# A hybrid decoder: the diagonal of linear attention from an elementwise product, the last output tile in two token halves, and dummy matmuls ahead of the first weights

## The chip, the cores and the metric

The kernel runs on one core of one Trainium2 chip. The metric is the device time of one launch in microseconds (us); lower is better. PE is the tensor engine, DVE the vector engine, ACT the scalar engine, SP the engine that issues most DMAs.

## What is computed

Two layers, each with two sub-layers on x (512 tokens, 1024 channels, float32), and a norm at the end:

```python
for l in range(DEPTH):                                   # DEPTH = 2
    x = x + hybrid_mixer(rmsnorm(x, norm1_w[l]), ...)    # SSD + gated linear attention + dilated attention
    x = x + conv_ffn(rmsnorm(x, norm2_w[l]), ...)        # up 1024 -> 2*2816, conv, SiLU gate, down 2816 -> 1024
return rmsnorm(x, final_norm_w)
```

The change touches two places of it. One is the gated linear attention (GLA): 4 heads with 64 key channels and 128 value channels, whose score for a token t and an earlier token s is the sum over the key channels of q[t] k[s] exp(b[t] - b[s]), b being the running sum of the log decays. For s = t the exponent is zero, so the diagonal of the scores is the plain product of q and k, summed over the 64 channels of the head. The other is the last FFN down-projection with the final norm: out[t] = x[t] * w / sqrt(mean(x[t]^2) + eps), where the mean runs over all 1024 channels.

## The kernel before

Channels lie on the 128 partitions and the 512 tokens on the free axis, so x is 8 tiles of 128x512 (`xs[m]`). Each float32 factor of a large product is split into a rounded part and a rest (`xh`, `xl` of the input, `wh`, `wl` of a weight), and each product is three matmuls, rounded by rounded, rounded by rest, rest by rounded: `mm3` puts them into a queue named `large`. `flush()` issues what the queue holds (L178). `mm()` (L186) and `transpose()` (L190) issue one small float32 matmul at once, and `follow()` then one large one (L183), so that small matmuls stand between large ones. PE's instructions stand in the order in which the program's text issues them; the other engines' order is set by a scheduler.

The weights come in units of 128x1024 (512 KB), 374 in all. `fetch` (L242) issues a unit's DMA on SP, up to 6 units ahead with 4 buffers; `parts` makes the rounded part on ACT (L249) and the rest on DVE (L251), up to 3 units ahead with 3 buffers. One unit is 24 large matmuls of 512 columns. `side()` registers a generator that goes on one step when a given number of units has been started; that is how attention, GLA and SSD are threaded between the projections.

GLA: `gla()` projects q and k for two pairs of heads (`gq`, `gk`, 128 channels are two heads of 64), then v and the output gate. `gla_pair()` (one for each pair, as a side) builds the score matrices `S` of the four 128-token blocks. Ahead of its levels it fills S with the diagonal: for each of two heads four matmuls k^T q over the 64 channels (8 of them a pair, 64 rows of PE in use), of which DVE keeps the diagonal by a multiply with the identity matrix (L620, 128x256, four a pair). Then nine levels follow. In a level, ACT makes decay factors (`ex`, L632), DVE multiplies q and k by them (`qsb`, `ksb`, L635 to L641), PE multiplies these (`mx<-qsb,ksb`), and DVE copies what belongs to the level into S (L649). Between the two pairs' groups of k^T q in layer 0 also four transposes of a 16-row tile `gd` stand on PE (L190), which SSD's decay needs.

The start: SP issues the DMAs of x's tiles and of the first weight units between them, then those of the constants. ACT makes `xh` of tile 0, after it has loaded its table, then `wh` of unit 0. PE runs three units of v projections, and then the sums `mx<-ones,acc` of the first norm, for which DVE has added up the squares of the eight x tiles in `acc` (L359), between the `wl` of the units and constants such as `lev`.

The end: the last loop makes the eight tiles of the down-projection, each 66 matmuls of 512 columns. Behind tile 7 come its two DVE steps (`dn`, then `x`), its square on ACT, sums on PE over the channels, the reciprocal root on DVE in 12 small instructions (`factors`), which also makes a diagonal matrix `dg` of the result; PE broadcasts it (`mx<-dg,ones`), DVE multiplies the eight tiles (L1069), and ACT and SP issue a DMA of 256 KB for each.

## Time and profile before

| | us |
|---|---|
| median of 3 runs (2321.18 to 2324.29) | 2322.52 |
| the profiled execution's own time | 2325.6 |
| its span, first to last instruction | 2323.8 |
| PE busy | 2300.8 (99%) |
| weight loads on PE | 1903.1 (82%) |
| DVE busy | 1420.4 (61%) |
| ACT busy | 917.6 (39%) |
| HBM traffic | 202.45 MB, 87 GB/s |

The mean granted clock of PE over the span is 0.995 of full speed. Busy times of PE are made of records that overlap, since matmuls are pipelined: what a matmul costs in a row of matmuls is the distance between two starts, and not the duration in its row. A float32 matmul is recorded as two (x2), since PE makes two passes for it. The rows are times in us from the start of the span; the bracket at a row's end is the idle time of its engine just ahead of it and what ended that.

### The profile page before, as it was taken

How to read it: one execution, taken by the hardware profiler on the slowest of the kernel's cores; microseconds unless marked ns; L12 is line 12 of the kernel's file. 1: busy time of each engine (PE TensorE's matmuls, PEld its weight loads, DVE VectorE, ACT ScalarE, POOL GpSimd, SP SyncE). 2: the span in 40 equal slices, each digit the busy share in tenths (PEclk: the TensorE clock that was granted, in tenths of full speed). 3: DMA queues.
4: the chain of work that ended last, by engine and by line, in shares of the span. 5: the costliest groups of instructions: out<-in, count | busy, mean ns of one | idle time of the engine just before them, and what ended most of it. 6: DMA issues, size and time to landing. Idle time of an engine off the chain costs nothing.

```text
span 2323.8 us, 27417 instructions
## 1 busy us (share of the span) xinstructions
PE 2300.8 (99%) x10776; PEld 1903.1 (82%) x10776; DVE 1420.4 (61%) x2527; ACT 917.6 (39%) x1503; POOL 0.2 (0%) x4
## 2 busy tenths in 40 slices
PE   8999999999999999999999999999999999999997
PEld 7888878888888888888888888788888888888886
DVE  5467548687865566654335764686888556665533
ACT  5354423445443333332244444234454433333321
POOL 0000000000000000000000000000000000000000
PEclk9999999999999999999999999999999999999998
DMA  5322222222223333333333222222222233323331
GB/s 182 105 77 82 73 64 87 78 72 73 82 73 100 92 99 95 96 100 94 97 91 100 83 82 73 71 84 73 73 73 82 82 95 96 97 94 100 98 93 54
DMA packets 58512, 204.21 MB, mean 88 GB/s; under 512 B 7152, under 2 KB 7824, under 8 KB 58384
## 3 DMA queue, kind: packets, MB, share of 16 engines
q1 hardware_dynamic: 57808, 201.42, 28.8%
q8 instruction: 84, 1.38, 0.2%
q10 hardware_dynamic: 576, 1.05, 0.1%
q14 instruction: 44, 0.36, 0.1%
HBM read 200.35 MB, written 2.10 MB: 87 GB/s over the span
## 4 chain that ended last, share of the span: by engine, by line
PE 98%; DVE 1%; ACT 0%; DMA 0%; issue 0%; DVEq 0%; SPq 0%; ACTq 0%
PE pp L178 77%; PE pp L183 11%; PE mx L186 8%; PE mx L190 2%; DVE wl L251 0%; DVE x L1069 0%; DVE cv L775 0%; DMA x<-in_xT 0%; DVE xD L834 0%; DVE th L918 0%; DVE th L943 0%; DVE xdt L833 0%; DVE xe L836 0%; ACT cx L778 0%; ACT L350 0%
## 5 line engine op out<-in xcount | busy, mean ns | idle before, releaser
L249 ACT CAST wh<-raw 128x1024 fp32r<-128x1024 f32 x374 | 393.1, 1051 | 952.7 <-PE pp L178 727.9
L251 DVE TENSOR_TENSOR wl<-raw,wh 128x1024 fp32r<-128x1024 f32 x374 | 457.4, 1223 | 355.6 <-ACT wh L249 350.1
L178 PE MATMUL pp<-xh,wl 128*128 128x512 f32 x1582 | 617.7, 390 | 0.0
L178 PE MATMUL pp<-xl,wh 128*128 128x512 f32 x1556 | 607.0, 390 | 0.0
L178 PE MATMUL pp<-xh,wh 128*128 128x512 f32 x1504 | 587.8, 391 | 0.0
L178 PEld LDWEIGHTS pp<-xh,wl 128*128 128x128 f32 x1582 | 297.7, 188 | 63.5 <-issue 1.0
L178 PEld LDWEIGHTS pp<-xl,wh 128*128 128x128 f32 x1556 | 293.1, 188 | 60.5 <-issue 0.5
L178 PEld LDWEIGHTS pp<-xh,wh 128*128 128x128 f32 x1504 | 283.3, 188 | 60.4 <-DVE wl L251 1.5
L183 PE MATMUL pp<-xh,wh 128*128 128x512 f32 x304 | 148.3, 488 | 0.0
L178 PE MATMUL pp<-hh,wl 128*128 128x512 f32 x352 | 136.9, 389 | 0.0
L178 PE MATMUL pp<-hh,wh 128*128 128x512 f32 x352 | 136.9, 389 | 0.0
L178 PE MATMUL pp<-hl,wh 128*128 128x512 f32 x352 | 136.9, 389 | 0.0
L771 DVE TENSOR_TENSOR cx<-pp,rstdB 128x512 f32<-128x512 f32 x76 | 52.3, 689 | 121.1 <-PE pp L178 121.0
L183 PE MATMUL pp<-xl,wh 128*128 128x512 f32 x252 | 124.6, 495 | 0.0
L183 PE MATMUL pp<-xh,wl 128*128 128x512 f32 x226 | 111.4, 493 | 0.0
L178 PE MATMUL pp<-wh,xh 128*128 128x512 f32 x245 | 96.3, 393 | 7.9 <-ACT wh L249 7.9
L178 PE MATMUL pp<-wh,xl 128*128 128x512 f32 x264 | 103.4, 392 | 0.0
L778 ACT ACTIVATE cx<-cv 128x512 f32<-128x512 f32 x76 | 48.1, 632 | 139.6 <-DVE cv L775 138.8
L178 PE MATMUL pp<-wl,xh 128*128 128x512 f32 x258 | 101.2, 392 | 0.5 <-DVE wl L251 0.5
L178 PE MATMUL pp<-wh,xr 128*128 128x512 f32 x255 | 78.7, 389 | 0.0
L178 PEld LDWEIGHTS pp<-hl,wh 128*128 128x128 f32 x352 | 66.1, 188 | 13.8
L178 PEld LDWEIGHTS pp<-hh,wl 128*128 128x128 f32 x352 | 66.1, 188 | 13.7
(275 smaller groups left out, 3542.6 us busy)
## 6 DMA issues: line engine op xcount, KB each, us to landing
raw<-in_wall SPq DMA_DIRECT2D x374, 512.0 KB, 3.6
x<-in_xT SPq DMA_DIRECT2D x8, 256.0 KB, 6.0
out_dram<-x ACTq DMA_DIRECT2D x4, 256.0 KB, 2.3
out_dram<-x SPq DMA_DIRECT2D x4, 256.0 KB, 2.5
cosR<-in_rope SPq DMA_DIRECT2D x2, 256.0 KB, 4.6
sinR<-in_rope SPq DMA_DIRECT2D x2, 256.0 KB, 4.8
amask<-in_amask SPq DMA_DIRECT2D x1, 256.0 KB, 5.3
levf<-in_lev SPq DMA_DIRECT2D x1, 224.0 KB, 3.7
```

The lines of the kernel that those rows point to most:

```text
L178: PE.matmul(o, lhsT=l, rhs=r, start=start, stop=stop)
L183: PE.matmul(o, lhsT=l, rhs=r, start=start, stop=stop)
L186: PE.matmul(o, lhsT=l, rhs=r, start=start, stop=stop)
L190: PE.transpose(o, i, idn)
L249: A.copy(h, r)
L251: V.tensor_sub(lo, r, f(h))
L771: V.tensor_mul(x, o, rstdB)
L778: A.activation(x, v, AF.Tanh)
```

## The change

1. **GLA's diagonal.** A new side, `gla_diagonal`, starts one unit after a pair's k projection: DVE multiplies q by k (`gqk`, 128x512). One unit later PE multiplies each 128-token block of it by a matrix of two columns that selects the channels of each head (four float32 matmuls with 128 rows and 2 columns, each followed by one large matmul), and DVE copies the result, 128x8, to `dia`. `gla_pair` fills S by two DVE multiplies of the identity by `dia`, 128x512 each. The 8 matmuls over 64 channels and the four multiplies of 128x256 are gone. `own64`, the constant that holds the selectors, is 22 columns wide and not 20. This happens for two pairs in each of two layers.
2. **The end.** Tile 7 of the last layer is made in two halves of 256 tokens, so that its 66 matmuls of 512 columns are 132 of 256. Between the matmuls of the second half stand the first half's sums (two after k = 1, two after k = 5), and after k = 13 two float32 matmuls of 128 columns that broadcast the factors (the factors' column, stepped by zero, against the identity; there is no `dg`). DVE makes the first half's steps, factors and eight multiplies of 128x256 in that time, and ACT and SP issue eight DMAs of 128 KB. Behind the second half the same follows for its 256 tokens.
3. **The start.** Unit 0's weights come by two DMAs of 256 KB, which ACT issues ahead of everything else; the second one stands behind a table load and a Tanh of one column. PE makes 17 float32 matmuls of `ones` by `ones`, 128 columns each, whose result isn't used. Unit 0's rounded part and rest are made in halves of 512 columns.

The first place is PE's row in layer 0 where the first pair starts (`gd` is the 16-row tile, `gq`, `gk` the pair's q and k; `xh`, `xl`, `wh`, `wl` as above). Before:

```order
L183 MATMUL pp_2601<-xh_104,wl_2515 128x512
L186 MATMUL mx_2631<-gq_2135,gk_2168 128x128
L183 MATMUL pp_2601<-xh_105,wh_2513 128x512
L186 MATMUL mx_2631<-gq_2135,gk_2168 128x128
L183 MATMUL pp_2601<-xl_113,wh_2513 128x512
L190 MATMUL mx_2649<-mats,gd_2011 128x16
L183 MATMUL pp_2601<-xh_105,wl_2515 128x512
```

and now:

```order
L179 MATMUL pp_2491<-wl_2525,xh_130 128x512
L179 MATMUL pp_2491<-wh_2524,xl_138 128x512
L191 MATMUL mx_2670<-mats,gd_2034 128x16
L184 MATMUL pp_2642<-xh_123,wh_2554 128x512
L191 MATMUL mx_2670<-mats,gd_2034 128x16
L184 MATMUL pp_2642<-xl_131,wh_2554 128x512
L191 MATMUL mx_2670<-mats,gd_2034 128x16
```

The matmuls of q by k are gone; the transposes of `gd` stay, and stand behind matmuls of 512 columns. The second place is PE's row farther ahead, where the second pair's k projection starts (`pp_2223` before, `pp_2249` after). Before:

```order
L178 MATMUL pp_2170<-xh_110,wl_2026 128x512
L178 MATMUL pp_2223<-xh_103,wh_2140 128x512
L178 MATMUL pp_2223<-xl_111,wh_2140 128x512
L178 MATMUL pp_2223<-xh_103,wl_2142 128x512
L178 MATMUL pp_2223<-xh_104,wh_2140 128x512
```

and now, with the four new matmuls of the first pair, whose weights are blocks of `gqk` and whose moving operand is two columns of `own64`:

```order
L179 MATMUL pp_2194<-xh_130,wl_2048 128x512
L187 MATMUL mx_2256<-own_99,gqk_2222 128x2
L184 MATMUL pp_2249<-xh_123,wh_2163 128x512
L187 MATMUL mx_2256<-own_99,gqk_2222 128x2
L184 MATMUL pp_2249<-xl_131,wh_2163 128x512
L187 MATMUL mx_2256<-own_99,gqk_2222 128x2
```

Four of the large matmuls that were issued in one row now each stand behind a small one. The third place is PE's last rows (`hh`, `hl` are the two parts of the FFN's hidden tiles). Before:

```order
L178 MATMUL pp_17541<-hh_16906,wh_17524 128x512
L178 MATMUL pp_17541<-hl_16907,wh_17524 128x512
L178 MATMUL pp_17541<-hh_16906,wl_17526 128x512
L186 MATMUL mx_17613<-ones,acc_16910 128x1 x4
L186 MATMUL mx_17613<-ones,sq_17611 128x1 x4
L186 MATMUL mx_17647<-dg_17642,ones 128x512
```

and now, first the place in the second half where the first half's squares are summed, then the last rows:

```order
L179 MATMUL pp_17553<-hl_15764,wh_17479 128x256
L179 MATMUL pp_17553<-hh_15763,wl_17480 128x256
L187 MATMUL mx_17554<-ones,sq_17625 128x1 x2
L179 MATMUL pp_17553<-hh_15839,wh_17507 128x256
L179 MATMUL pp_17553<-hl_15840,wh_17507 128x256
```

```order
L179 MATMUL pp_17553<-hh_16917,wh_17535 128x256
L179 MATMUL pp_17553<-hl_16918,wh_17535 128x256
L179 MATMUL pp_17553<-hh_16917,wl_17536 128x256
L187 MATMUL mx_17555<-ones,acc_16921 128x1 x2
L187 MATMUL mx_17555<-ones,sq_17741 128x1 x2
L187 MATMUL mx_17765<-mats,rs 128x128 x2
```

The first half's sums stand between matmuls of the second half; behind the last large matmul are the sums, and two broadcasts, of 256 tokens. The diff:

```diff
--- before.py
+++ after.py
@@ -120,7 +120,8 @@
     is_b = (i[:, None] // 32 == np.arange(4)[None, :]).astype(f)
     own = np.stack([is_r, is_b], axis=1)
     own64 = np.concatenate([i[:, None] % 16 == np.arange(16)[None, :],
-                            i[:, None] % 64 // 16 == np.arange(4)[None, :]], axis=1).astype(f)
+                            i[:, None] % 64 // 16 == np.arange(4)[None, :],
+                            i[:, None] // 64 == np.arange(2)[None, :]], axis=1).astype(f)
     lev = np.zeros((P, 7, 64), f)
     for n in range(7):
         L = 1 << n
@@ -246,9 +247,11 @@
         while len(units) < min(n, len(plan)):
             r = raws[len(units)]
             h = wgt_p.tile([P, 1024], F32R, tag="wh", name=nm("wh"))
-            A.copy(h, r)
             lo = wgt_p.tile([P, 1024], F32R, tag="wl", name=nm("wl"))
-            V.tensor_sub(lo, r, f(h))
+            e = 1024 if units else 512
+            for i in range(0, 1024, e):
+                A.copy(h[:, i:i + e], r[:, i:i + e])
+                V.tensor_sub(lo[:, i:i + e], r[:, i:i + e], f(h)[:, i:i + e])
             units.append((h, lo))
 
     def unit(kind):
@@ -305,7 +308,7 @@
         gws.append(cp.tile([16, 256], F32, name=f"gw{l}"))
     fnw = cp.tile([P, KD], F32, name="fnw")
     ident, tri, strict = mats[:, 0], mats[:, 1], mats[:, 2]
-    own64 = cp.tile([P, 20], F32, name="own64")
+    own64 = cp.tile([P, 22], F32, name="own64")
     own_c = cp.tile([P, 4, P], F32R, name="own_c")
     ones = cp.tile([P, P], F32, name="ones")
     V.memset(ones, 1.0)
@@ -323,6 +326,13 @@
         for n in range(7):
             V.tensor_copy(lev[:, n].rearrange("p (c i) -> p c i", c=4), levf[:, n:n + 1].to_broadcast([P, 4, 64]))
         V.tensor_copy(own_c, own64[:, 16:20].unsqueeze(2).to_broadcast([P, 4, P]))
+
+
+    warm = sml([P, 1], n="warm")
+    A.activation(warm, ones[:, 0:1], AF.Tanh)
+    w = mx()
+    for _ in range(17):
+        PE.matmul(w[:, :P], lhsT=ones, rhs=ones, start=True, stop=True)
 
     xh = [xp.tile([P, T], F32R, name=f"xh{m}") for m in range(KD)]
     xl = [xp.tile([P, T], F32R, name=f"xl{m}") for m in range(KD)]
@@ -571,11 +581,21 @@
             V.tensor_sub(p1, p1, p0)
         yield 1
 
+    def gla_diagonal(q, k, dia):
+
+        p = big([P, T], n="gqk")
+        V.tensor_mul(p, q, k)
+        yield 1
+        o = mx()
+        for c in range(4):
+            mm(o[:, 2 * c:2 * c + 2], p[:, blk(c)], own64[:, 20:22], True, True)
+        V.tensor_copy(dia, o[:, :8].rearrange("p (c j) -> p c j", j=2))
+
     def gla(l, gd, yh, yl):
         pc = pcs[l]
         las = []
         d = side(gla_decay(l, gd, las), 1)
-        qk = []
+        qk, dias = [], []
         for m in range(2):
             o = pp()
             proj_cm(o, xhl)
@@ -586,6 +606,9 @@
             k = big([P, T], n="gk")
             V.tensor_mul(k, o, rstdB)
             qk.append((q, k))
+            dia = lp.tile([P, 4, 2], F32, tag=f"dia{m}", name=nm("dia"))
+            dias.append(dia)
+            side(gla_diagonal(q, k, dia), 1)
         vt, wt = [], []
         o = proj_tm(blk)
         for c in range(4):
@@ -599,9 +622,9 @@
             V.scalar_tensor_tensor(w, w, 1.0, o[c], ALU.add, ALU.mult)
             wt.append(w)
         finish(d)
-        return [side(gla_pair(m, qk[m], las[m][1], vt, wt, pc, yh, yl), 1 + m) for m in range(2)]
-
-    def gla_pair(m, qk, cum, vt, wt, pc, yh, yl):
+        return [side(gla_pair(m, qk[m], dias[m], las[m][1], vt, wt, pc, yh, yl), 1 + m) for m in range(2)]
+
+    def gla_pair(m, qk, dia, cum, vt, wt, pc, yh, yl):
         q, k = qk
         suf = big([P, T], n="suf")
         V.memset(suf, 0.0)
@@ -612,13 +635,9 @@
         hp = [slice(0, 64), slice(64, 128)]
         S = [big([P, 2, 2, P], n="S") for _ in range(2)]
         X = []
-        for j in range(2):
-            o = mx()
-            for c in range(4):
-                mm(o[:, blk(c)], k[hp[j], blk(c)], q[hp[j], blk(c)], True, True)
-            for x in range(2):
-                V.tensor_mul(S[x][:, :, j], o[:, 256 * x:256 * x + 256].rearrange("p (c t) -> p c t", c=2),
-                             ident.unsqueeze(1).to_broadcast([P, 2, P]))
+        for x in range(2):
+            V.tensor_mul(S[x], ident.unsqueeze(1).unsqueeze(1).to_broadcast([P, 2, 2, P]),
+                         dia[:, 2 * x:2 * x + 2].unsqueeze(3).to_broadcast([P, 2, 2, P]))
         for n in range(9):
             L = 1 << n
             G = 256 // L
@@ -963,7 +982,7 @@
         nc.sync.dma_start(out=pcs[0], in_=ins["pc"][0])
         for m in range(KD):
             nc.sync.dma_start(out=xs[m], in_=ins["xT"][:, m])
-            if m in (0, 3, 7):
+            if m in (3, 7):
                 fetch(1 + (m + 1) // 4)
         constants()
         for m in range(KD):
@@ -974,6 +993,10 @@
             square(m, acc)
         side(norm_side(acc, True), 4)
 
+    raws.append(raw_p.tile([P, 1024], F32, tag="raw", name=nm("raw")))
+    for i in range(2):
+        s = slice(512 * i, 512 * i + 512)
+        A.dma_start(out=raws[0][:, s], in_=ins["wall"][0][:, s])
     for l in range(depth):
         pc = pcs[l]
         merged = [None] * KD
@@ -1032,7 +1055,7 @@
         acc = new_acc()
         end = l + 1 == depth
         idx = 0
-        for m in range(KD):
+        for m in range(KD - end):
             o = pp()
             for k in range(KF):
                 if idx % 8 == 0:
@@ -1047,27 +1070,79 @@
             V.tensor_add(xs[m], xs[m], t)
             if not end:
                 norm_split(m, pcs[l + 1][:, O_N1:O_N1 + 8])
-                square(m, acc)
-            elif m < KD - 1:
-                square(m, acc)
+            square(m, acc)
+            if end:
                 A.activation(xs[m], xs[m], AF.Copy, scale=fnw[:, m:m + 1])
         if not end:
             side(norm_side(acc, True), 2)
 
-    sq = big([P, T], n="sq")
-    A.activation(sq, xs[KD - 1], AF.Square)
-    ss = mx()
-    for c in range(4):
-        mm(ss[:, c:c + 1], acc[:, blk(c)], ones[:, 0:1], c == 0, False)
-    for c in range(4):
-        mm(ss[:, c:c + 1], sq[:, blk(c)], ones[:, 0:1], False, c == 3)
-    A.activation(xs[KD - 1], xs[KD - 1], AF.Copy, scale=fnw[:, KD - 1:KD])
-    dg = factors(ss, 4)
-    b = mx()
-    mm(b, ones, dg, True, True)
-    for m in range(KD):
-        V.tensor_mul(xs[m], xs[m], b)
-        (nc.sync if m % 2 else A).dma_start(out=out[:, m], in_=xs[m])
+
+
+    last, m = xs[KD - 1], KD - 1
+    wts = []
+
+    def half(h, k):
+        if not h:
+            if (idx + k) % 8 == 0:
+                run()
+                units_now[0] = unit("cm")
+            s = blk((idx + k) % 8)
+            wts.append((units_now[0][0][:, s], units_now[0][1][:, s]))
+        n = slice(256 * h, 256 * h + 256)
+        mm3(os[h][:, :256], wts[k], (hhl[k][0][:, n], hhl[k][1][:, n]), k == 0, k == KF - 1)
+
+    def sums(h, t, first):
+        for c in range(2):
+            mm(ssh[h][:, c:c + 1], t[:, blk(c if t is not acc else 2 * h + c)], ones[:, 0:1], first and c == 0,
+               not first and c == 1)
+
+    def finish_tile(h):
+        n = slice(256 * h, 256 * h + 256)
+        t = big([P, 256], n="dn")
+        V.tensor_mul(t, os[h][:, :256], rstdB[:, n])
+        V.tensor_add(last[:, n], last[:, n], t)
+        sq = big([P, 256], n="sq")
+        A.activation(sq, last[:, n], AF.Square)
+        A.activation(last[:, n], last[:, n], AF.Copy, scale=fnw[:, m:m + 1])
+        return sq
+
+    def factors_of(h):
+        t = sml([P, 2])
+        V.tensor_scalar(t, ssh[h][:, :2], 1.0 / D, EPS, ALU.mult, ALU.add)
+        rsqrt(rs[:, 2 * h:2 * h + 2], t, 2)
+
+    def store(h):
+        n = slice(256 * h, 256 * h + 256)
+        b = mx()
+        for c in range(2):
+            mm(b[:, blk(c)], rs[:, 2 * h + c:2 * h + c + 1].to_broadcast([P, P]), ident, True, True)
+        for i in range(KD):
+            V.tensor_mul(xs[i][:, n], xs[i][:, n], b[:, :256])
+            (nc.sync if i % 2 else A).dma_start(out=out[:, i, n], in_=xs[i][:, n])
+
+    os, ssh = [pp(), pp()], [mx(), mx()]
+    units_now = [(wh, wl)]
+    for k in range(KF):
+        half(0, k)
+    run()
+    sq = finish_tile(0)
+    for k in range(KF):
+        half(1, k)
+        if k == 1:
+            flush()
+            sums(0, acc, True)
+        elif k == 5:
+            flush()
+            sums(0, sq, False)
+            factors_of(0)
+        elif k == 13:
+            flush()
+            store(0)
+    flush()
+    sums(1, acc, True)
+    sums(1, finish_tile(1), False)
+    factors_of(1)
+    store(1)
     assert pos[0] == len(plan)
```

## Rows read from the trace of the kernel before

**Rows 1.** Page, part 4: share of the chain that ended last, by engine

```profile
PE 98%; DVE 1%; ACT 0%; DMA 0%; issue 0%; DVEq 0%; SPq 0%; ACTq 0%
```

**Rows 2.** Waits of PE: what it waited for: us in total, times, longest us

```profile
PE pp L178 <- ACT wh L249: 7.9, 1, 7.9
```

**Rows 3.** Timeline of PE, layer 0: start us, us, line, tiles, count

```profile
314.81 0.39 PE L178 MATMUL pp<-wl,xh 128*128 128x512 f32 x1
...
318.44 0.39 PE L178 MATMUL pp<-wh,xl 128*128 128x512 f32 x1
...
333.21 0.40 PE L178 MATMUL pp<-xh,wl 128*128 128x512 f32 x1
...
340.20 0.39 PE L178 MATMUL pp<-xh,wl 128*128 128x512 f32 x1
```

**Rows 4.** Tile gk, PE's instructions: duration ns min/median/max, first and last start

```profile
L186 PE MATMUL mx<-gq,gk x64: 272/322/373, 318.8 to 1486.9; 64*128 64x128 f32 x64
```

**Rows 5.** Timeline of PE, layer 0, between the two groups

```profile
329.03 0.63 PE L178 MATMUL pp<-xh,wh 128*128 128x512 f32 x1
...
332.75 0.39 PE L178 MATMUL pp<-xh,wh 128*128 128x512 f32 x1
```

**Rows 6.** Windows: us; busy of PE, PEld, DVE, ACT, POOL; PEclk, DMA, GB/s

```profile
324.00:334.00 10.00, 10.00 (x29) 6.38 (x28) 1.62 (x6) 0.59 (x1) 0.00 (x0) 0.66 0.08 32
1476.00:1480.00 4.00, 4.00 (x11) 3.20 (x12) 0.00 (x0) 0.00 (x0) 0.00 (x0) 0.57 0.00 0
276.00:280.00 4.00, 4.00 (x25) 3.16 (x24) 2.23 (x2) 2.03 (x3) 0.00 (x0) 1.00 0.25 44
```

**Rows 7.** Timeline of PE, first norm's sums

```profile
26.59 0.28 PE L186 MATMUL mx<-ones,acc 128*128 128x1 f32 x2
...
27.04 0.28 PE L186 MATMUL mx<-ones,acc 128*128 128x1 f32 x2
```

**Rows 8.** Timeline of DVE and PE, first and later GLA level

```profile
334.82 0.85 DVE L635 TENSOR_TENSOR qsb<-gq,ex 64x256 f32<-64x256 f32 x2 [8.68 <-ACT ex L632]
...
343.85 0.38 PE L186 MATMUL mx<-qsb,ksb 128*128 128x128 f32 x2
...
368.54 0.42 DVE L641 TENSOR_TENSOR ksb<-gk,ex 128x256 f32<-128x256 f32 x1
...
370.18 0.38 PE L186 MATMUL mx<-qsb,ksb 128*128 128x128 f32 x2
```

**Rows 9.** Timeline of DVE and PE, the kernel's end

```profile
2306.10 0.95 PE L186 MATMUL mx<-ones,acc 128*128 128x1 f32 x8
...
2306.30 0.69 DVE L1046 TENSOR_TENSOR dn<-pp,rstdB 128x512 f32<-128x512 f32 x1 [11.52 <-PE pp L178]
...
2309.94 0.16 DVE L374 TENSOR_SCALAR s<-mx 128x4 f32<-128x4 f32 x1 [2.22 <-PE mx L186]
...
2312.31 0.87 DVE L380 TENSOR_SCALAR dg<-mats,rs 128x128 f32<-128x128 f32 x4
...
2313.24 2.08 PE L186 MATMUL mx<-dg,ones 128*128 128x512 f32 x2 [3.34 <-DVE dg L380]
...
2315.36 4.87 DVE L1069 TENSOR_TENSOR x<-x,mx 128x512 f32<-128x512 f32 x8 [2.17 <-PE mx L186]
```

**Rows 10.** Page, part 5: a weight load's group: busy us, mean ns

```profile
L178 PEld LDWEIGHTS pp<-hh,wl 128*128 128x128 f32 x352 | 66.1, 188 | 13.7
```

**Rows 11.** Timeline of ACT, PE and DVE, the kernel's start

```profile
4.92 1.28 ACT L350 ACT_TABLE_LOAD   x1 [4.92 <-DMA x<-in_xT]
...
9.18 0.79 PE L178 MATMUL pp<-wl,xh 128*128 128x512 f32 x1 [0.46 <-DVE wl L251]
...
11.48 0.51 PE L178 MATMUL pp<-wh,xh 128*128 128x512 f32 x1
...
19.45 1.50 DVE L324 CAST lev<-levf 128x256 uint8<-128x256 f32 x7 [0.68 <-DMA levf<-in_lev]
...
25.14 0.69 DVE L359 TENSOR_TENSOR acc<-acc,sq 128x512 f32<-128x512 f32 x1
```

## The prediction

> **What bounds the kernel now.** I read the chain that ended last first: 98% of it is PE [rows 1]. Then PE's waits: the only long one is 7.9 us for the first weights [rows 2]; the rest of its idle time lies in the last 17 us. So between 9.2 and 2306.3 us a microsecond counts if PE issues one less, and DVE and ACT count only where they would make PE wait. The timeline gives the price of the common instruction: 16 distances between matmuls of 512 columns take 318.44 - 314.81 = 3.63 us, 0.227 each [rows 3]. Last I read the granted clock in windows, to see where PE runs below full speed, and the two ends of the kernel by themselves.
>
> **1. GLA's diagonal: what goes.** In the second group of layer 0, nine large matmuls (the one at 333.21 and the eight that follow the small ones) and eight products of 64 rows lie between 333.21 and 340.20: 6.99 us [rows 3]. Less 9 x 0.227 = 2.04, the eight cost 4.95. There are 64 records at two passes each, so 32 products, four groups [rows 4]: 4 x 4.95 = **19.8 us**, all on PE's row, hence on the path.
>
> Behind the first group of each layer the granted clock is low: 0.66 over 324 to 334 us, 0.57 over 1476 to 1480 [rows 6]. That is 10 x 0.34 + 4 x 0.43 = 5.1 us of full clock lost. The matmuls do not quite double: the nine distances from 329.03 to 332.75 take 3.72 us for 2.04 [rows 5], so a low microsecond loses 0.45 where half a clock would be 0.50, and the price is 5.1 x 0.9 = 4.6 us. What the engine did before was the group of products on half its rows, with four transposes of a 16-row tile at its end. The transposes stay; the products go. Does the clock then hold? A stretch that also has transposes in it, 276 to 280, has a clock of 1.00 [rows 6]. So transposes alone are not seen to do it; with the products gone I take the whole **4.6** as gained, bounds 0 and 4.6. The Trainium skill, TensorE: Matmul & The Clock Gate, Part 4 (PE-mode transpose), says that a transpose does not count as work for the clock in the way that a matmul does. By that rule the dips could stay with the transposes, and the sum would be 4.6 less; the window at 1.00 speaks against it.
>
> **What comes.** Sixteen small matmuls (four for each of four pairs). Nearest row: sums with one column, each followed by a large one, stand 27.04 - 26.59 = 0.45 apart [rows 7], less 0.227 = 0.225 each: **3.6 us**. The bound above is the price of what goes, 0.62 each (4.95 / 8), 9.9 us; below nothing is excluded, since each issues two passes. I take the near end: these too have all 128 rows and next to no columns. On DVE, per pair, `gqk` (0.69, as `dn` with the same shape [rows 9]), a copy of 8 columns and two multiplies of 512 columns (1.4) come, four multiplies of 256 columns (0.42 each, as in 334.82's two [rows 8]) go: about +0.5 us, in a stretch where DVE idles.
>
> **Who is late next.** PE reaches the first level earlier by its 2 x 4.95 and 10 x 0.34 x 0.9 = 3.1, 13.0 us, in layer 0. In the rows before, `qsb` is ready at 334.82 + 0.85 = 335.67 and PE takes it at 343.85: 8.2 us of cover [rows 8]. That would leave a wait of 4.8. But `qsb` itself waited 8.68 us for ACT's `ex`, which stands on ACT behind a weight cast that waits for PE's release of a buffer; it moves with PE. With that the levels come out nearly level with PE, and in the later ones the cover is 370.18 - (368.54 + 0.42) = 1.2 us each [rows 8]. I put **0.5 us** of new wait in all, bounds 0 and 2 x 4.8 = 9.6. GLA sums to 19.8 + 4.6 - 3.6 - 0.5 = **20.3 us**.
>
> **2. The end.** Before, 17.5 us lie between the start of `dn` at 2306.30 and the end of the span at 2323.8 [rows 9]. After, for 256 tokens: `dn` and the add 0.45 each (0.42 by the 256-column row plus a handover); square and sums 1.3 (square 0.42; four passes at low clock; before, square and eight passes filled most of 2306.30 + 1.4 to 2309.94); the twelve small DVE instructions unchanged, 2312.31 - 2309.94 = 2.4; no `dg` (0.87 goes); broadcast of four passes of 128 columns for two of 512, half of 2.08, 1.1; eight multiplies at 0.34 (4.87 / 8 = 0.61 is 0.08 less than one's 0.69; 0.42 less 0.08), 2.75; from the last multiply to the end as before, 2323.8 - 2320.23 = 3.5. Sum 11.95, so **5.55 us** gained. The eight early DMAs are issued some 5 us ahead of the late ones, and no queue has to wait for them.
>
> Against it, on PE in the second half: four sums of one column, eight passes, 0.95 [rows 9], and two broadcasts of 128 columns, four passes, 0.5: **1.45**. And 132 matmuls of 256 columns for 66 of 512. Half of 0.227 is 0.113, but a weight load takes 0.188 in its row [rows 10]; what two successive loads cost is shown by the sums, eight passes with a load each in 0.95 us, 0.119 apiece [rows 9]. I take 0.12: 132 x 0.12 - 66 x 0.227 = **+0.9**. Cover for the first half's own chain: its sums come after 18 matmuls (2.2 us) and need `dn`, add and square, 1.3; its factors have 24 matmuls (2.9 us) for 2.4. Tight, but without a wait; up to 0.7 if a handover is longer. End: 5.55 - 1.45 - 0.9 = **3.2 us**, bounds +5.5 and -2.
>
> The Trainium skill, TensorE: Matmul & The Clock Gate, Part 3 (Packing small matmuls), states that weight loads overlap matmuls in flight only where their row groups differ. Here all are on the same 128 rows, and loads of 0.188 disappear inside 0.227, so the trace disagrees for 512 columns; for 256 no row shows it. The rule's result is rival C.
>
> **3. The start.** Before, ACT loads its table at 4.92, when tile 0 has landed, for 1.28 us; PE's second matmul is at 9.18, and until 11.48 five distances take 2.30 us for 1.13 at full speed [rows 11]. Table, first half cast and dummies could bring PE forward by 1.3 + 0.5 + 0.5 and give back the 1.2 of low clock: 3 us or a little more. But all of that ends at the sums of the first norm at 26.59 [rows 7], which need `acc`, ready at 25.14 + 0.69 = 25.83 [rows 11]. DVE gets there through `lev`, which waited for its DMA until 19.45; the constants' DMAs are issued in the same order, and one DMA less on SP ahead of them brings them some 0.5 forward. So the sums can't start much before 25.2, and PE, which is there at about 23, waits 2 us. Gain 26.59 - 25.2 = **1.3 us**, rounded down; bounds 3.5 if `acc` comes sooner, and -1.5 if the clock falls in the wait and the next stretch pays what 9.18 to 11.48 paid. The dummies themselves, 34 passes, 3.8 us at full speed and 7.6 at half, end before the first weights or barely behind them.
>
> **Sum.** 20.3 + 3.2 + 1.3 = **24.8 us**. The profiled execution took 2325.6, so 2300.8; against the median of 2322.5, **2297.7**.
>
> **Rivals.**
>
> A, the levels become the bound. DVE and ACT between two level matmuls do not move with PE, and each layer's pairs lose up to 4.8 us: 9.6 instead of 0.5, 2306.8. For it: the cover of 1.2 us per level. Against: 8.68 us of DVE's idle time is ended by ACT, which itself waits for PE. 15%.
>
> B, the dips stay, since the transposes stay: 2297.7 + 4.6 = 2302.3. For it: the clock falls where they stand, in both layers. Against: 276 to 280. 18%.
>
> C, loads don't hide behind 256 columns. Then a matmul is 0.188 + 0.113 = 0.301, 132 of them 39.7 for 15.0: +24.7 where I have +0.9, so 2321.5, within 0.2%. If the clock falls as well with PE computing a third of the time, both double, 0.60: +64.5, **2361, slower**. It decides from 132 p = 15.0 + 25.7 + 4.6, p = 0.343 us per matmul. For it: 0.188 is longer than 0.113. Against: 0.119 per load and pass in the sums. 2% for each of the two.
>
> D, the change does less than it says at both ends: the first half's chain makes PE wait, and the start is gated by `acc` with a low clock behind it: -2 and -1.5 for 3.2 and 1.3, 2305.7. 6%. On the other side, E, the start is not gated and the early norm costs nothing: 2.2 at the start and 2.3 at the end, 2293. 7%.
>
> **How the numbers follow.** The forecast has 50%, A 15, B 18, C 4, D 6, E 7. The range takes in A, B, D and E: 2292 to 2307.5, which leaves out C and the tails of A and E. A measurement of this kernel tells about 0.2%, 4.6 us, from no change. All cases but C lie more than 15 us below the median: faster 0.95; same 0.03 (C at full clock, and several small misses together); slower 0.02.
>
> **What would show it.** GLA right: no matmul of 64 rows on PE, sums of `gqk` about 0.45 apart with their followers, clock 1.00 where it was 0.66 and 0.57, and PE's waits for `qsb`, `ksb` under 1 us. Rival A shows there as waits on DVE, B as a granted clock near 0.5 behind the transposes. The end right: starts of 256-column matmuls 0.12 apart, and about 12 us from the last of them to the end of the span; 0.3 apart is C. The start right: a PE wait of about 2 us on `acc` ahead of the first sums, at about 25 us; no wait and sums at 23 is E. The prediction is wrong if PE's row no longer sets the time in the middle, or if a split matmul costs more than 0.12.

## The result, and the profile after

| | before | after |
|---|---|---|
| median, us | 2322.52 | 2304.07 |
| lowest to highest | 2320.32 to 2324.29 | 2300.78 to 2304.75 |
| profiled execution, span | 2323.8 | 2301.5 |
| mean granted clock of PE | 0.995 | 0.997 |

The ratio is 0.9916 (95% interval 0.9903 to 0.9929): 18.4 us less. The forecast was 24.8 less, 2297.7; the time lies in its range. The profiled pair differs by more, 22.3 us of span, and that difference turns out to be a finding and not noise (below).

The page of the changed kernel, its totals and the chain that ended last, to be read beside [rows 1]:

```profile
PE 2287.3 (99%) x10850; PEld 1904.6 (83%) x10850; DVE 1424.3 (62%) x2546; ACT 920.3 (40%) x1507; POOL 0.2 (0%) x4
...
PE 96%; DVE 3%; DMA 1%; issue 0%; ACT 0%; SPq 0%; DVEq 0%; ACTq 0%
```

PE still sets the time. Its waits in the changed kernel (us in total, times, longest us):

```profile
PE mx L187 <- DVE rs L354: 2.4, 1, 2.4
...
PE mx L187 <- DVE acc L369: 1.1, 1, 1.1
...
PE mx L335 <- DVE ones L314: 1.0, 1, 1.0
...
PE pp L179 <- ACT wh L253: 0.6, 1, 0.6
...
PE pp L179 <- DVE wl L254: 0.4, 1, 0.4
```

PE's own list has no wait for `qsb` or `ksb`: the GLA levels did not become the bound. Its weight loads (PEld) have a list of their own, and there each layer has two short waits that the kernel before does not have, 0.4 us for `ksb` and 0.4 us for `ac`, a tile of SSD's decay. The first of them in layer 0:

```profile
341.25 0.30 PEld L187 LDWEIGHTS mx<-qsb,ksb 128*128 128x128 f32 x2 [0.38 <-DVE ksb L657]
```

New on PE are a wait for `acc` ahead of the first norm's sums, and one for `ones` ahead of the dummies, which costs nothing.

Since PE's row holds nearly the same matmuls in both kernels, each matmul of the one can be set beside the same one of the other, and the difference of their starts tells where time was won or lost. Neighbouring matmuls agree to some 0.02 us; over long stretches the lead also drifts by a few tenths. A positive lead means that the changed kernel is ahead:

| place (us of before) | lead of after | step | forecast step |
|---|---|---|---|
| behind the start, 262 | -1.92 | -1.9 | +1.3 |
| behind layer 0's new small matmuls, 282 | -3.72 | -1.8 | -1.8 |
| behind layer 0's 64-row groups, 341 | +9.09 | +12.8 | 9.9 and 3.1 of clock |
| behind the first levels, 365 | +8.87 | -0.2 | -0.25 |
| ahead of layer 1's, 1412 | +9.03 | +0.2 | 0 |
| behind its new small matmuls, 1431 | +7.22 | -1.8 | -1.8 |
| behind its 64-row groups, 1487 | +18.65 | +11.4 | 9.9 and 1.5 of clock |
| behind its first levels, 1513 | +18.15 | -0.5 | -0.25 |
| last large matmul, 2306 | +16.14 | -2.0 | -2.35 |
| end of the span | +22.3 | +6.2 | +5.55 |

At 370 us the lead has gone down to 8.59, and at 645 it is 8.75: the two waits of the weight loads cost 0.5 us in each layer, and some of it comes back by 1412.

**GLA.** The new small matmuls of layer 0, on PE's timeline:

```profile
265.89 0.39 PE L179 MATMUL pp<-xh,wl 128*128 128x512 f32 x1
...
266.12 0.28 PE L187 MATMUL mx<-own,gqk 128*128 128x2 f32 x2
...
266.57 0.28 PE L187 MATMUL mx<-own,gqk 128*128 128x2 f32 x2
...
267.02 0.28 PE L187 MATMUL mx<-own,gqk 128*128 128x2 f32 x2
...
267.48 0.28 PE L187 MATMUL mx<-own,gqk 128*128 128x2 f32 x2
...
267.93 0.39 PE L179 MATMUL pp<-xl,wh 128*128 128x512 f32 x1
```

They stand 0.45 apart with their followers, as the sums of [rows 7] did, so 0.225 each. The granted clock where the 64-row groups stood (windows; PEclk is the number behind POOL), to be read beside [rows 6]:

```profile
318.00:330.00 12.00, 12.00 (x53) 9.14 (x52) 8.59 (x13) 4.58 (x7) 0.00 (x0) 1.00 0.30 88
1460.00:1472.00 12.00, 12.00 (x52) 9.30 (x52) 9.86 (x20) 3.90 (x6) 0.00 (x0) 1.00 0.16 46
```

**The end.** Two rows that are 15 matmuls of 256 columns apart, and the chain behind the last large matmul:

```profile
2273.78 0.28 PE L179 MATMUL pp<-hh,wl 128*128 128x256 f32 x1
...
2275.58 0.28 PE L179 MATMUL pp<-hh,wl 128*128 128x256 f32 x1
...
2290.16 0.42 DVE L1102 TENSOR_TENSOR dn<-pp,rstdB 128x256 f32<-128x256 f32 x1
...
2292.18 0.16 DVE L1111 TENSOR_SCALAR s<-mx 128x2 f32<-128x2 f32 x1 [1.15 <-PE mx L187]
...
2294.57 0.89 PE L187 MATMUL mx<-mats,rs 128*128 128x128 f32 x4 [2.42 <-DVE rs L354]
...
2295.50 2.74 DVE L1120 TENSOR_TENSOR x<-x,mx 128x256 f32<-128x256 f32 x8 [0.99 <-PE mx L187]
```

1.80 / 15 = 0.120 a matmul. From `dn` at 2290.16 to the end of the span are 11.3 us, where before had 17.5 [rows 9].

**The start.** PE's timeline around the first norm's sums, and the clock around them, to be read beside [rows 7, 11]:

```profile
24.23 0.39 PE L179 MATMUL pp<-wh,xl 128*128 128x512 f32 x1
...
25.72 0.38 PE L187 MATMUL mx<-ones,acc 128*128 128x1 f32 x2 [1.10 <-DVE acc L369]
...
26.28 0.28 PE L187 MATMUL mx<-ones,acc 128*128 128x1 f32 x2
...
30.76 0.63 PE L179 MATMUL pp<-wh,xl 128*128 128x512 f32 x1
...
31.19 0.63 PE L179 MATMUL pp<-wh,xh 128*128 128x512 f32 x1
```

```profile
24.00:26.00 2.00, 0.90 (x6) 0.47 (x4) 1.93 (x3) 1.34 (x2) 0.00 (x0) 1.00 0.88 258
28.00:36.00 8.00, 8.00 (x25) 6.62 (x25) 5.22 (x22) 7.26 (x8) 0.00 (x0) 0.57 0.25 83
```

PE idles 1.1 us ahead of the sums, and the clock is still 1.00 there. Over 28 to 36 it is 0.57 in the mean (a half from 28.5 to 35.3): 30.76 to 31.19 is 0.43 for one matmul of 512 columns, where the kernel before paid 0.227 at this place. What PE and `acc` wait for is seen on ACT and DVE:

```profile
6.07 0.72 ACT L360 ACTIVATE xh<-x,pc 128x512 fp32r<-128x512 f32 x1 [3.40 <-DMA x<-in_xT]
...
18.96 1.51 DVE L327 CAST lev<-levf 128x256 uint8<-128x256 f32 x7 [0.26 <-DMA levf<-in_lev]
...
22.75 1.05 ACT L253 CAST wh<-raw 128x1024 fp32r<-128x1024 f32 x1 [1.36 <-DMA raw<-in_wall]
...
23.84 1.23 DVE L254 TENSOR_TENSOR wl<-raw,wh 128x1024 fp32r<-128x1024 f32 x1 [0.23 <-ACT wh L253]
...
24.98 0.69 DVE L369 TENSOR_TENSOR acc<-acc,sq 128x512 f32<-128x512 f32 x1
```

### The profile page after: what moved, and what is told of

Same layout as the page of the kernel before. It is cut to its first block, busy times and chain, and to the rows that moved or that the text cites. A ratio compares the mean times of both kernels' runs of the same rounds, so it can differ in the third digit from the quotient of the medians.

```text
span 2301.5 us, 27603 instructions
## 1 busy us (share of the span) xinstructions
PE 2287.3 (99%) x10850; PEld 1904.6 (83%) x10850; DVE 1424.3 (62%) x2546; ACT 920.3 (40%) x1507; POOL 0.2 (0%) x4
## 3 DMA queue, kind: packets, MB, share of 16 engines
q10 hardware_dynamic: 1440, 1.57, 0.2%
## 4 chain that ended last, share of the span: by engine, by line
PE 96%; DVE 3%; DMA 1%; issue 0%; ACT 0%; SPq 0%; DVEq 0%; ACTq 0%
PE pp L179 76%; PE pp L184 11%; PE mx L187 8%; PE mx L191 2%; DVE wl L254 1%; DVE S L668 0%; DMA mats<-in_mats 0%; DMA raw<-in_wall 0%; DMA x<-in_xT 0%; DVE qsb L654 0%; DVE cv L794 0%; DVE th L937 0%; DVE p L684 0%; DVE mg L959 0%; DVE x L1120 0%
## 5 line engine op out<-in xcount | busy, mean ns | idle before, releaser
L253 ACT CAST wh<-raw 128x1024 fp32r<-128x1024 f32 (+1 forms) x375 | 393.3, 1049 | 919.7 <-PE pp L179 699.6
L254 DVE TENSOR_TENSOR wl<-raw,wh 128x1024 fp32r<-128x1024 f32 (+1 forms) x375 | 457.8, 1221 | 351.6 <-ACT wh L253 346.5
L179 PE MATMUL pp<-hh,wh 128*128 128x512 f32 (+1 forms) x374 | 141.0, 377 | 0.0
L179 PE MATMUL pp<-hl,wh 128*128 128x512 f32 (+1 forms) x374 | 140.8, 376 | 0.0
L179 PE MATMUL pp<-hh,wl 128*128 128x512 f32 (+1 forms) x374 | 140.8, 376 | 0.0
L179 PEld LDWEIGHTS pp<-hh,wh 128*128 128x128 f32 x374 | 70.4, 188 | 12.9
L179 PEld LDWEIGHTS pp<-hl,wh 128*128 128x128 f32 x374 | 70.4, 188 | 12.8
```

The costliest lines, as they stand in the source:

```text
L179: PE.matmul(o, lhsT=l, rhs=r, start=start, stop=stop)
L253: A.copy(h[:, i:i + e], r[:, i:i + e])
L254: V.tensor_sub(lo[:, i:i + e], r[:, i:i + e], f(h)[:, i:i + e])
```

## Experiments

**The three parts by themselves, and two of them together.** In the first run only the GLA hunks are taken:

```diff
-                mm(o[:, blk(c)], k[hp[j], blk(c)], q[hp[j], blk(c)], True, True)
...
+            side(gla_diagonal(q, k, dia), 1)
```

> Only the GLA part of the change, on the kernel before. Theory (read from the two traces, aligned matmul by matmul): the GLA part is worth 20.5 us (12.4 + 11.0 where the 64-row products stood, less 2.8 for the sixteen new small matmuls and less than 1 us of waits), so 2302 against 2322.5. Rival: the median moved by only 18.5 where the profiled pair moved by 22.3, because part of the GLA gain exists only in some executions (the low clock comes back in others): then 2306 or more.

Measured: 2307.19, ratio 0.9933 (0.9920 to 0.9945), 14.5 us less than the 2321.7 of the kernel before on the same chip. That is the rival's side, and by more than it said. The low clock did not come back: in this kernel's trace all windows around 315 to 335 and 1455 to 1475 read 1.00, and its executions lie close together, 2306.05 to 2307.30, where those of the kernel before lay at 2320.72 to 2325.62 on the same chip. So the spread of the kernel before goes with the code that was replaced; what was too large is what the low clock costs an average execution of it. About 1 us more is lost in this kernel by an accident of DVE's order:

```profile
263.62 1.23 DVE L252 TENSOR_TENSOR wl<-raw,wh 128x1024 fp32r<-128x1024 f32 x1 [0.24 <-ACT wh L250]
...
264.87 0.68 DVE L578 TENSOR_TENSOR gqk<-gq,gk 128x512 f32<-128x512 f32 x1
...
265.65 0.35 PE L187 MATMUL mx<-own,gqk 128*128 128x2 f32 x2 [0.85 <-PE pp L179]
```

The scheduler put `gqk` behind the rest of a weight unit, which waits for ACT, and PE waits 0.85 for it (the row names PE as the releaser, since DVE's start is close by; `gqk` ends at 265.55). In the whole change `gqk` starts at 261.95 and there is no such wait. 19.8 - 3.6 - 0.7 around the levels - 1.1 is 14.4: the row prices without any low clock.

Only the end:

```diff
-        for m in range(KD):
+        for m in range(KD - end):
...
+    for k in range(KF):
+        half(0, k)
```

> Only the token halves of the last tile with the early norm, on the kernel before. Theory: worth 4.2 us, so 2318.3. Rival: the 132 matmuls with the inserted sums eat the gain, and 1 us or less is left: 2321.5 or more.

Measured: 2319.40, ratio 0.9989 (0.9980 to 0.9998), 2.3 less by the medians; the interval reaches from 0.5 to 4.6 and tells the theory from the rival only weakly. The pair of GLA and end against GLA alone, below, gives 4.6.

Only the start:

```diff
+    raws.append(raw_p.tile([P, 1024], F32, tag="raw", name=nm("raw")))
...
+        A.dma_start(out=raws[0][:, s], in_=ins["wall"][0][:, s])
...
+    for _ in range(17):
+        PE.matmul(w[:, :P], lhsT=ones, rhs=ones, start=True, stop=True)
```

> Only the start part (unit 0's halves on ACT's queue, early table load, 17 dummy matmuls), on the kernel before. Theory: it loses 2.4 us, since PE arrives at the first norm's sums before their input, waits about 1 us, and the granted clock falls to a half some 3 us later for some 7 us: 2324.9, with that wait and that clock in the trace. Rival: the start gains the 1.3 us that was forecast, and the loss in the changed kernel comes from elsewhere: 2321.2.

Measured: 2324.92, ratio 1.0007 (0.9998 to 1.0016), with executions from 2319.80 to 2326.95. By the medians it loses 3.2, by the interval nothing certain. Its trace has the wait for `acc` (2.9 us) and the low clock behind it:

```profile
26.79 0.38 PE L186 MATMUL mx<-ones,acc 128*128 128x1 f32 x2 [2.88 <-DVE acc L368]
```

```profile
28.00:36.00 8.00, 8.00 (x27) 6.76 (x27) 3.26 (x18) 6.28 (x7) 0.00 (x0) 0.57 0.37 125
324.00:334.00 10.00, 10.00 (x38) 6.20 (x38) 4.39 (x10) 0.51 (x1) 0.00 (x0) 1.00 0.18 52
1474.00:1480.00 6.00, 6.00 (x24) 3.93 (x23) 0.81 (x3) 0.84 (x1) 0.00 (x0) 1.00 0.00 0
```

The last two windows hold something else. This kernel has the GLA code of the kernel before, the same 64-row groups and transposes, and there the clock is 1.00, where [rows 6] had 0.66 and 0.57. With only the end changed it is 0.83 and 1.00 in the same windows. So the low clock behind the 64-row groups comes in some executions and not in others: it stands in three of the six places that these three traces have, and in none of the eighteen places of the nine traces with the new GLA code. Set beside the kernel before, matmul by matmul as above, this one also gives the price of the two dips, since the instructions are the same: its lead goes from -3.00 to -0.05 across the first and from -0.05 to +1.52 across the second, 2.95 and 1.57 us. The times of the kernel before on this chip go with the mean granted clock of each execution: 2320.72 to 2322.09 at 0.997, 2322.92 to 2324.32 at 0.996, 2325.40 and 2325.62 at 0.995; the profiled one, 2325.6, has 0.995.

The change without its start:

```diff
-    for _ in range(17):
-        PE.matmul(w[:, :P], lhsT=ones, rhs=ones, start=True, stop=True)
...
-        A.dma_start(out=raws[0][:, s], in_=ins["wall"][0][:, s])
```

> The change without its start part. Theory: 2.4 us faster than the whole change, about 24.7 below the kernel before: 2297.8. Rival: the start part gains 1.3, so that this one is slower than the whole change by that: 2305.4 beside its 2304.1.

Measured: 2302.58, ratio 0.9914 (0.9901 to 0.9928). It is 1.5 below the whole change (by medians taken on different chips), so the theory has the sign; it misses the size, for 24.7 below the kernel before were expected and 19.1 were measured on this chip. This kernel carries the 0.85 us wait for `gqk` too, which the whole change does not have. Against GLA alone it is 4.6 lower on the same chip.

**What of the start loses.** The whole change without the dummies:

```diff
-    w = mx()
-    for _ in range(17):
-        PE.matmul(w[:, :P], lhsT=ones, rhs=ones, start=True, stop=True)
```

> The whole change without the 17 dummy matmuls. Theory: in the changed kernel PE reaches the first norm's sums 1.1 us before their input is ready, and this wait is followed by a stretch at half clock that costs about 3 us. Without the dummies the first matmuls run at half clock, PE reaches the sums some 1.2 us later, about when the input is ready, and the later stretch stays at full clock: about 2302, 2 us faster than the whole change at 2304. Rival: the half clock at 28 us has another cause (the small sums, the DMA traffic), the dummies only help: 2305 or more.

Measured: 2300.98, ratio 0.9906 (0.9893 to 0.9920); all executions between 2300.45 and 2301.45. It is 3.1 faster than the whole change, and 3.9 faster than its repetition on this chip (below). But the mechanism that I had given is not quite what the trace shows:

```profile
8.46 0.63 PE L179 MATMUL pp<-wh,xl 128*128 128x512 f32 x1
...
8.89 0.63 PE L179 MATMUL pp<-wh,xh 128*128 128x512 f32 x1
...
26.25 0.38 PE L187 MATMUL mx<-ones,acc 128*128 128x1 f32 x2 [0.85 <-DVE acc L366]
...
34.14 1.02 PE L187 MATMUL mx<-dg,ones 128*128 128x512 f32 x2
```

```profile
28.00:36.00 8.00, 8.00 (x36) 6.66 (x37) 5.24 (x22) 8.00 (x10) 0.00 (x0) 1.00 0.31 107
```

PE does not come later than `acc`; it comes 0.8 later than in the whole change and still waits 0.85 us, against 1.10, and the clock stays at 1.00. Two readings are left. Either the dummies and a wait bring the clock down together, or the length of the wait alone decides, and the dummies count only because they bring PE to the sums earlier. All traces fit the second: behind waits of 1.10, 1.95 (the repetition) and 2.88 us (only the start) there is a stretch at half clock, behind 0.85 us here, and 0.74 and 0.76 us for `rstdB` in the last two runs, there is none, and the runs below have long waits without dummies. No two runs have the same wait at the sums with and without dummies, so at this place neither reading is shown.

Real work in the wait: 8 large matmuls of the next unit are issued ahead of the sums, and 12 ahead of the broadcast:

```diff
+        for _ in range(8 if early else 0):
+            follow()
         dg = norm_stats(acc, both)
         yield 1
+        for _ in range(12 if early else 0):
+            follow()
```

> The whole change, and ahead of the first norm's sums PE issues 8 of the next unit's large matmuls (1.8 us of real work), and 12 ahead of the broadcast that follows, so that PE reaches both after their input. Theory: no wait, no low clock, and the start gives 2.1 us where it lost 2.4: 2299.7. Rival: the low clock comes without a wait, because the sums themselves are small work: no faster than 2303.

Measured: 2309.06, ratio 0.9941 (0.9929 to 0.9954), slower than the whole change, and slower than either side had it. The first half of the idea works: the sums start at 25.99 without a wait, and the clock is 1.00 from 28 to 36. The second half puts matmuls ahead whose input `xr` is not there yet, the broadcast then waits for ACT's `v`, and PE has two new waits:

```profile
PE mx L187 <- ACT v L426: 4.6, 1, 4.6
...
PE pp L184 <- ACT xr L416: 2.1, 1, 2.1
```

> As the run before, without the 17 dummy matmuls. It tells what the dummies are worth where nothing behind them waits. Theory: 1.2 us, the low clock of the first matmuls: 2300.9. Rival: nothing, because the sums' input sets the time anyway: the same as with them.

Measured: 2310.86, with the same two waits (4.6 and 2.1), so neither side came. Here a stretch at half clock comes without any dummies (0.58 over 40 to 48; with the dummies, in the run before, 0.57):

```profile
40.00:48.00 8.00, 5.11 (x10) 3.40 (x11) 0.00 (x0) 5.14 (x8) 0.00 (x0) 0.58 0.00 0
```

So with the same waits the clock falls with dummies and without. The dummies are worth 1.8 where they don't meet a wait at the sums, though under these waits that is no clean measure.

**What brings the low clock behind the 64-row groups.** The kernel before, with the transposes of `gd` two units later:

```diff
-        sd = side(ssd_decay(l, gd, dec), 1)
+        sd = side(ssd_decay(l, gd, dec), 3)
```

> The kernel before, with SSD's four 16-row transposes moved two units on, away from the group of 64-row products. In the kernel before, single executions spread from 2320.3 to 2325.6 with a mean clock of 0.997 to 0.995, and the dips behind the first groups are there in the profiled one. Theory: the 64-row products alone bring them: the same spread and median, 2321.7. Rival: it takes the transposes directly behind the products: all executions near 2320.5 at 0.997, no dip in the trace.

Measured: 2321.19, ratio 0.9995 (0.9985 to 1.0004). The profiled execution has a clock of 1.00 over 324 to 334 and over 1474 to 1480, and the upper part of the spread is gone: 2320.20 to 2322.58, beside 2320.68 to 2325.43 of the kernel before on the same chip. The one trace says little, since the trace of the start alone has no dip either; the ten executions say more: all have a mean clock of 0.997, where 8 of 15 of the kernel before have 0.996 or 0.995. That is the rival's picture, though the median is not at its 2320.5: it takes the products with the transposes directly behind them, and then it happens in some executions.

**Taking away what the start waits for.** The whole change once more, for the spread:

> The whole change once more, on the same chip as the two runs behind it. Theory: most executions have the stretch at half clock behind the sums and lie at 2303 to 2305, a few don't and lie near 2301. Rival: the spread has nothing to do with the start, and the executions without the dummies would spread in the same way.

Measured: 2304.85, ratio 0.9925 (0.9912 to 0.9937), 2304.19 to 2305.64; the wait for `acc` was 1.9 us in this trace and the clock 0.50 from 28 to 36. None of these was near 2301.

Then the casts of `lev` are registered as a side, so that DVE's scheduler finds the additions of squares ahead of them:

```diff
-        for n in range(7):
-            V.tensor_copy(lev[:, n].rearrange("p (c i) -> p c i", c=4), levf[:, n:n + 1].to_broadcast([P, 4, 64]))
+        def levels():
+            for n in range(7):
+                V.tensor_copy(lev[:, n].rearrange("p (c i) -> p c i", c=4), levf[:, n:n + 1].to_broadcast([P, 4, 64]))
+            return
+            yield
+
+        side(levels(), 6)
```

> The whole change, and the casts of the constant lev registered six units later, so that DVE's scheduler puts the last additions of squares ahead of the weights' rests: acc should be ready near 22.5 and not at 25.7. Theory: acc gates the start, so PE no longer waits at the sums, comes there at 24.5, and the clock holds: 2299.2, 4.9 less than the whole change. Rival: the dummies alone bring the clock down at 28 us, or the broadcast dg gates in acc's place: 2302 or more.

Measured: **2299.66**, ratio 0.9902 (0.9889 to 0.9916), 2299.29 to 2299.86: 5.2 less than the whole change on the same chip, and the fastest version. The casts and the last addition on DVE, and PE's row, with one matmul of the kernel before to set beside it:

```profile
19.71 0.29 DVE L328 CAST lev<-levf 128x256 uint8<-128x256 f32 x1 [1.26 <-DMA levf<-in_lev]
...
22.33 0.69 DVE L374 TENSOR_TENSOR acc<-acc,sq 128x512 f32<-128x512 f32 x1
...
23.86 0.28 PE L187 MATMUL mx<-ones,acc 128*128 128x1 f32 x2
...
31.95 1.02 PE L187 MATMUL mx<-dg,ones 128*128 128x512 f32 x2
...
35.79 0.50 PE L179 MATMUL pp<-wh,xr 128*128 128x512 f32 x1 [0.74 <-ACT rstdB L403]
...
36.13 0.40 PE L179 MATMUL pp<-wl,xr 128*128 128x512 f32 x1
```

```profile
37.53 0.39 PE L178 MATMUL pp<-wl,xr 128*128 128x512 f32 x1
```

The granted clock in the kernel with the casts moved:

```profile
28.00:36.00 8.00, 7.26 (x30) 5.37 (x31) 7.01 (x26) 3.85 (x5) 0.00 (x0) 1.00 0.35 129
```

`acc` is ready at 23.02 and not at 25.67, the sums start at 23.86 without a wait, and with the dummies in place the clock holds at 1.00. Four of the seven casts still stand between the additions, and the levels' constant still waits for its DMA until 19.71. Next in line is a wait of 0.7 for `rstdB`; behind it this kernel leads the one before by 1.4 us (the same matmul at 37.53 before and at 36.13 now), where the forecast gave 1.3 to the start.

> As the run before, without the 17 dummy matmuls. Theory: PE reaches the sums at 25.2, the low clock of its first matmuls being the only difference: 2299.9, 0.7 more than with the dummies and 1.1 less than the whole change without dummies (2301.0). Rival: without a gate the dummies are worth the whole 1.2 us, or nothing.

Measured: 2301.58, ratio 0.9910 (0.9896 to 0.9923). Without a wait the dummies are worth 1.9 us: with them the first matmuls run at full clock, without them at the low one. With the wait they cost 3.1 to 3.9 (2304.07 and 2304.85 against 2300.98). Against no_dummies the earlier `acc` brought nothing (2301.58 and 2300.98): the sums start 0.5 earlier there, and a wait for `rstdB` takes it back.

## Why the forecast was right, and where it was off

**What bounds, and the GLA terms: right.** PE's row set the time, and the table above gives the terms back: 24.2 us where 19.8 + 4.6 were forecast, 3.6 for the small matmuls where 3.6, 0.7 around the levels (1.0 with what is lost up to 370 us) where 0.5. Rival A did not come in its size: `qsb` moved with the weight cast on ACT, from 334.82 to 330.70, and PE's first level still finds it ready. It is near, though: the second level's weight load waits 0.38 for `ksb`. Rival B did not come: the transposes still stand there, in a row of large matmuls, and the clock is 1.00 in all nine traces with the new GLA code. The Trainium skill, TensorE: Matmul & The Clock Gate, Part 4 (PE-mode transpose), has it that a transpose does not count as work for the clock in the same way; that dips follow from it at this place is not borne out.

**The term that was mis-sized: the low clock, 4.6.** It was priced rightly for the one execution in which it was read (4.5 by the start alone, 2.95 + 1.57) and taken off the median. The profiled execution of the kernel before, at 2325.6, is 3.1 us above the median, among the slowest of its executions (2320.32 to 2325.89 over all comparisons), and it is one in which the dips stand in full. Other traces with the same GLA code have them in part or not at all. A typical execution had about 4.6 - 3.1 = 1.5 of it to give back, if the dips are what sets the times apart, as the mean clocks say; GLA alone gave 14.5, what the row prices give without it. The subtraction of 3.1 for the median was right as arithmetic and wrong as a sum: what sets the profiled execution apart was, by its mean clock, the very thing that the change removes. That is 3.1 of the 6.4 us that are missing.

**The step that failed: the start, +1.3.** That `acc` gates it was right: `acc` was ready at 25.67 where I had 25.2. The casts of `lev` do come 0.5 earlier (18.96 for 19.45), as forecast, but the last addition stands behind the rest of a weight unit, which waits for ACT's `wh`, which waits 1.36 for its DMA, and only 0.16 of the 0.5 is left. That PE then waits was right too, though it comes at 24.6 and not at 23: tile 0's data landed at 6.07 and not at 4.92, and PE's lead at 11.48 was 2.0 and not 3. What I had as a bound only, that the clock falls behind the wait and the next stretch pays, is what all three traces with dummies and this wait show (the whole change twice, the start alone): 31.19 to 35.03 at 0.43 a matmul. The step is -1.9, and 3.2 us are missing there. The experiment with the earlier `acc` shows that the 1.3 was there to be had (1.4 there).

**The end: right, a little too low.** 0.120 a matmul of 256 columns as taken from the sums; +4.2 where 3.2 was forecast. The chain was 11.3 for 11.95, some 0.2 less each at the sums (at full clock, where I had the low one), at the broadcast and behind the last multiply; the inserted work cost 2.0 for 2.35. Rival C is out: weight loads of 0.19 hide behind matmuls at 0.12. The rule of the Trainium skill, TensorE: Matmul & The Clock Gate, Part 3 (Packing small matmuls), that loads overlap only where row groups differ, does not hold here.

So the ledger from the forecast to the median: 24.8, less 3.2 at the start, plus 1.0 at the end, less 0.3 in GLA, is 22.3, the profiled pair; less 3.1 for the low clock that the median execution of before did not have, less 0.8 because the profiled execution of the changed kernel lies that far below its median, 18.4.

What stays open is whether the dummies have a part in the half clock behind the wait, or only the length of the wait, and what decides whether an execution has the dips behind the 64-row groups.

## What to carry to other kernels

Before a stretch at low clock is booked as a gain, look whether the profiled execution stands above the median: what makes it slow may be just that stretch, and then the median has no such gain to give. Warming an engine up ahead of the work can bring it sooner to a wait further on, and the wait can cost more than the warming gave; here moving a constant's casts on another engine turned the same dummies from a loss of over 3 us into a gain of nearly 2. And where work is put forward to fill a wait, its own inputs have to be looked up first.

## What the runs showed of the hardware that was not expected

A wait of 1.1 us at a full granted clock was followed, some 3 us later, by 7 us at half clock (25.72, 28.5 to 35.3), though PE was busy all the while. After a wait of 1.95 us at the same place the half clock came within 0.5 us of its end and lasted 10 us; a wait of 0.85 us, without the dummies, was followed by none; and waits of 2.1 and 4.6 us without dummies had 7 us of it. And the same instructions, products on 64 rows with 16-row transposes behind them, ran at 0.66 in one execution, at 0.83 in another, and at 1.00 in a third.
